# Splitting the first loads in halves and laying the two running column groups out as one piece per k-tile, in a two-layer trunk kernel

## The chip, the cores and the metric

The kernel runs on one core of a Trainium2 chip. The metric is the device time of one execution in microseconds. TensorE multiplies, VectorE and ScalarE do elementwise work and read accumulators, GpSimd is all but unused, and SyncE (SP) issues every DMA from one queue, in the order of the program.

## The reference

A decoder trunk of two layers works on 256 tokens of width 2048, in float32. The begin of the kernel, which the change touches, is the modulated input of layer 0 and its first product:

```python
def _adaln(c, w, b):
    mod = jax.nn.silu(c) @ w + b
    shift, scale, gate = jnp.split(mod, 3, axis=-1)
...
h = x * (1 + scale) + shift          # layer 0
proj = h @ in_w                      # 2048 x 10304: z 4096, x 4096, B 1024, C 1024, dt 64
z, xBC, dt = jnp.split(proj, ...)
xBC = silu(causal_depthwise_conv(xBC))
...                                  # chunked state-space scan, gated RMSNorm, y @ out_w
```

Behind it come a shared key/value product, a layer of dilated window attention, and two layer norms.

## The kernel before, in words

**Precision and pieces.** Each product of float32 matrices is done in three passes over operands split in a high and a low half. A weight piece `raw` is 128x1024 (512 KB): for the products here 2 k-tiles of 128 rows, 512 columns each. `load_piece` fetches it, `split` makes `whi` on ScalarE (L99) and `wlo` on VectorE (L101). `cm_piece` (L125 to L127) takes the weights as the stationary operand: 24 matmuls of 128x256 for a piece, 12 for each k-tile. `tm_piece` (L173 to L175) has the tokens as the stationary operand: 12 matmuls of 128x512.

**The stage at the begin (0 to about 187 us).** It makes h, k-tile by k-tile (16 of them), and at the same time starts products with the k-tiles that are there. `c` is broadcast to all partitions and goes through SiLU (`cb_`, L68). For each k-tile, two loads `araw` (128x2048, 1024 KB; scale and shift) are multiplied by `cb_` and summed along the row by one instruction of VectorE, the dot (`ada_dot`, L251); `ada_bias` adds the bias table `adab` (L256); `htmp` (L413) applies scale and shift to x on ScalarE; `actT` (L414) is h's high half and L415 its low half, on VectorE. `xt` holds x for two k-tiles. `h_step` is one dot with what follows from it; it is called a set number of times for each weight piece.

**The written order.** The pieces are worked in an order written out as rows of words:

```python
for row in ("b4:0. b6:0. h z2:0. b2:0 x1:0 h", "b2:1. x1:1. z1:0 z1:1. z4:0 h h",
```

`b4:0` is piece 0 of a product that was begun for column group b4; a dot ends what is accumulated for now, and `put_away` copies or adds the accumulators to SBUF (L486, L488). `h` stands for the two running column groups (the first bc group and the first xs group), whose accumulators `first` stay in PSUM for the whole stage: an `h` takes the next piece of one group or of the other, in turn, so that each piece covers two k-tiles of one group. `fetch_piece` issues the load of the next piece in this order, `fetch` that of the next `araw`; both go into SP's one queue. `split` is called one piece ahead. After the stage the convolutions of the two running groups are done (`conv`, L320 and L323).

Of the kernel before, what the change touches and what calls it, by code (L numbers as in the profile page):

```python
# [13 lines left out]
ALU = mybir.AluOpType  # L14
# [35 lines left out]
def trunk(ctx, tc, xT, x, c, par, cst, bias, lnrow, ada, wdt, win, wxs, wout, wk, wv, wbin, wbout, out):  # L50
# [16 lines left out]
    bcast(cb_, c)  # L67
    S.activation(cb_, cb_, AF.Silu)  # L68
# [221 lines left out]
    with ExitStack() as cA:  # L290
# [14 lines left out]
        with ExitStack() as cS:  # L305
# [4 lines left out]
            begun = {("z", 0): (win[6], 6, szt[0]), ("z", 1): (win[7], 4, szt[1]),  # L310
                     ("xs", 1): (win[5], 4, as_cm(y[0])), ("bc", 2): (win[1], 4, as_cm(y[1])),
                     ("z", 2): (win[8], 14, y[2]), ("bc", 4): (win[2], 12, as_cm(y[3])), ("z", 4): (win[10], 6, y[4]),
                     ("bc", 6): (win[3], 12, as_cm(y[5])), ("z", 6): (win[12], 10, y[6]), ("z", 5): (win[11], 8, y[7])}
# [39 lines left out]
            def product(kind, g, pre=None):  # L353

                if kind == "xs" and g > 1:
                    return xs_wide(g)

                src, k0, part = begun.get((kind, g), (None, 0, None))
                if src is None:
                    src = win[{"bc": g // 2, "xs": 4 + g, "z": 6 + g}[kind]]  # L360
                if kind == "z":
                    ps = tm_chunk(src, hh_, hl_, rate=R, k0=k0, pre=pre)
                    if g not in sz:
                        sz[g] = p0.tile([P, 2, 512], F32, name="sz")
                    for b in range(2):
                        if part is not None:
                            V.tensor_tensor(part[:, b, :], ps[b], part[:, b, :], op=ALU.add)
                        S.activation(sz[g][:, b, :], part[:, b, :] if part is not None else ps[b], AF.Silu)
                    return
                ps = cm_quad(src, hhi, hlo, rate=R, k0=k0)  # L370
                t = tiles(ps)
                if part is not None:
                    for w in range(2):
                        V.tensor_tensor(part[:, 2 * w:2 * w + 2, :], ps[w], part[:, 2 * w:2 * w + 2, :], op=ALU.add)
                    t = [part[:, n, :] for n in range(4)]
                if kind == "xs":
                    xs_conv(g, t)
                else:
                    bc_conv(g, t)

            with ExitStack() as c0:
# [6 lines left out]
                def fetch():  # L388
                    i = len(raws)
                    if i < len(cols):  # L390
                        raws.append(ada_load((wp1, pe)[i // 2 % 2], *cols[i]))

# [4 lines left out]
                def h_step():  # L397
# [6 lines left out]
                    ada_dot(0, kind, kt, raw)  # L404
                    if kt > 1:
                        pin[0] = None
                    fetch()
                    while late:
                        late.pop()()
                    if kind == "shift":  # L410
                        ada_bias(0, slice(kt, kt + 1), slice(0, 2))
                        t = pe.tile([P, L], F32, name="htmp")
                        S.activation(t, xts[kt // 2][:, kt % 2, :], AF.Identity, bias=shift(0, kt), scale=scale(0, kt))  # L413
                        S.activation(hhi[:, kt, :], t, AF.Copy)  # L414
                        late.append(lambda: V.tensor_tensor(hlo[:, kt, :], t, hhi[:, kt, :].bitcast(F32),  # L415
                                                            op=ALU.subtract))
# [7 lines left out]
                for row in ("b4:0. b6:0. h z2:0. b2:0 x1:0 h", "b2:1. x1:1. z1:0 z1:1. z4:0 h h",  # L424
# [10 lines left out]
                source = {"dt": wdt, -2: win[0], -1: win[4], **{n: p[0] for n, p in zip(names, begun.values())}}  # L435
                pss = {-2: first[0], -1: first[1]}
# [53 lines left out]
                begin, done, ended, halves = {}, set(), [], {}  # L490
                for i, (k, q, ends) in enumerate(order):
                    fetch_piece()
                    if i == 16:
# [11 lines left out]
                    z = str(k)[0] == "z"  # L505
# [4 lines left out]
                    if z:  # L510
# [527 lines left out]
def _layout(x, c, ada_w, ada_b, ln_g, ln_b, a_in_w, a_conv_w, a_conv_b, a_dt_bias,  # L1038
# [29 lines left out]
    def mask(delta, win_, dil):  # L1068
# [11 lines left out]
    win = _pieces(np.concatenate([bc, xs[:, :1024], z], 1))  # L1080
# [3 lines left out]
        "ada": ada, "wdt": _dt(dt), "win": win, "wxs": _pieces(xs[:, 1024:], 256, 4),  # L1084
# [23 lines left out]
```

## Time and profile before

| | |
|---|---|
| median of 3 runs | 1255.73 us (1254.37 to 1255.77) |
| profiled execution | 1254.31 us |
| its span, first to last instruction | 1252.5 us |
| TensorE busy | 1218.5 us (97%) |
| VectorE busy | 1032.4 us (82%) |
| ScalarE busy | 702.1 us (56%) |
| granted TensorE clock, mean | 0.998 |
| first matmul | 14.96 us after the span's start |

Times in the profile are counted from the span's first instruction. A row of a timeline has the start, the duration, the engine, the line of the source, the operation, and in brackets how long the engine was idle before it and what it waited for.

### The profile page before, as it was taken

The numbers are of one execution on the slowest core, as the hardware profiler recorded it, in microseconds if no ns is written. First come the engines' busy times: TensorE is split into PE (matmuls) and PEld (weight loads), VectorE is DVE, ScalarE is ACT, GpSimd is POOL, SyncE is SP. The second block draws the span as 40 slices with busy tenths as digits, with TensorE's granted clock in tenths as the row PEclk, the third lists the DMA queues.
The fourth block names the chain that finished last, engine by engine and source line by source line (L and its number), as shares of the span: only waits on it lengthen the run. The fifth ranks groups of instructions, "written<-read, shape, count | busy, mean of one in ns | idle before, by whom it ended". The sixth has DMA issues, their size and how long they took to land.

```text
span 1252.5 us, 18746 instructions
## 1 busy us (share of the span) xinstructions
PE 1218.5 (97%) x7086; PEld 1042.7 (83%) x7086; DVE 1032.4 (82%) x1466; ACT 702.1 (56%) x1039; POOL 0.2 (0%) x4
## 2 busy tenths in 40 slices
PE   4999999999999999999999999999999999999997
PEld 4989998898888878788888788888888888888886
DVE  6999986999987989899777778879888866758777
ACT  3655577869588789653444444434445644445631
POOL 0000000000000000000000000000000000000000
PEclk9999999999999999999999999999999999999999
DMA  9999977677556546699898569989998774464741
GB/s 381 422 421 423 420 252 261 225 274 286 201 169 225 171 159 202 223 328 358 335 323 298 174 192 383 363 315 344 364 389 309 229 248 136 132 203 120 228 177 67
DMA packets 80586, 335.88 MB, mean 268 GB/s; under 512 B 9104, under 2 KB 9328, under 8 KB 67696
## 3 DMA queue, kind: packets, MB, share of 16 engines
q1 hardware_dynamic: 80496, 334.69, 73.9%
q8 instruction: 55, 0.90, 0.3%
q14 instruction: 35, 0.29, 0.1%
HBM read 332.47 MB, written 2.18 MB: 267 GB/s over the span
## 4 chain that ended last, share of the span: by engine, by line
PE 86%; DVE 5%; DMA 5%; issue 2%; ACT 1%; SPq 0%; DVEq 0%; ACTq 0%
PE acc L149 20%; PE acc L174 13%; PE acc L175 13%; PE acc L173 13%; PE acc L152 10%; PE acc L125 3%; PE acc L127 3%; PE acc L126 3%; DMA raw<-in_wk 2%; DVE wlo L101 1%; PE py L625 1%; DMA raw<-in_win 1%; DVE araw L251 1%; DMA araw<-in_ada 1%; DMA raw<-in_wv 1%
## 5 line engine op out<-in xcount | busy, mean ns | idle before, releaser
L99 ACT ACTIVATE whi<-raw 128x1024 fp32r<-128x1024 f32 x392 | 412.1, 1058 | 386.0 <-PE acc L175 151.4
L101 DVE TENSOR_TENSOR wlo<-raw,whi 128x1024 fp32r<-128x1024 f32 x392 | 473.5, 1221 | 145.3 <-ACT whi L99 141.1
L149 PE MATMUL acc<-actT,whi 128*128 128x512 f32 x1280 | 405.2, 397 | 0.0
L152 PEld LDWEIGHTS acc<-actT,wlo 128*128 128x128 f32 x1280 | 238.9, 188 | 62.8 <-DVE wlo L101 8.2
L174 PE MATMUL acc<-wlo,actT 128*128 128x512 f32 x688 | 270.0, 392 | 0.6 <-DVE wlo L101 0.5
L173 PE MATMUL acc<-whi,actT 128*128 128x512 f32 x688 | 266.6, 394 | 1.2 <-ACT actT L681 1.2
L152 PE MATMUL acc<-actT,wlo 128*128 128x256 f32 x1280 | 253.7, 280 | 4.5 <-DVE wlo L101 3.7
L251 DVE SCALAR_TENSOR_TENSOR araw<-araw,cb__72 128x2048 f32<-128x2048 f32 x96 | 219.3, 2285 | 9.5 <-DMA araw<-in_ada 9.3
L149 PEld LDWEIGHTS acc<-actT,whi 128*128 128x128 f32 x1280 | 195.8, 189 | 0.4
L175 PE MATMUL acc<-whi,actT 128*128 128x512 f32 x432 | 168.8, 391 | 0.0
L174 PEld LDWEIGHTS acc<-wlo,actT 128*128 128x128 f32 x688 | 129.3, 188 | 28.5 <-DVE wlo L101 2.8
L173 PEld LDWEIGHTS acc<-whi,actT 128*128 128x128 f32 x688 | 128.8, 188 | 27.2 <-ACT actT L681 1.7
L125 PE MATMUL acc<-actT,whi 128*128 128x256 f32 x384 | 108.9, 288 | 17.6 <-ACT actT L414 17.5
L126 PE MATMUL acc<-actT,whi 128*128 128x256 f32 x384 | 109.5, 287 | 0.0
L127 PE MATMUL acc<-actT,wlo 128*128 128x256 f32 x384 | 107.3, 287 | 1.2 <-DVE wlo L101 1.2
L175 PE MATMUL acc<-whi,ylo 128*128 128x512 f32 x256 | 100.7, 393 | 0.0
L175 PEld LDWEIGHTS acc<-whi,actT 128*128 128x128 f32 x432 | 81.1, 188 | 16.6
L125 PEld LDWEIGHTS acc<-actT,whi 128*128 128x128 f32 x384 | 74.3, 194 | 18.6 <-ACT actT L414 17.7
L126 PEld LDWEIGHTS acc<-actT,whi 128*128 128x128 f32 x384 | 75.1, 196 | 0.3
L127 PEld LDWEIGHTS acc<-actT,wlo 128*128 128x128 f32 x384 | 73.9, 196 | 1.6 <-DVE wlo L101 1.6
L175 PEld LDWEIGHTS acc<-whi,ylo 128*128 128x128 f32 x256 | 48.1, 188 | 9.7
L583 ACT ACTIVATE seg<-cbc,cumT 128x128 f32<-128x128 f32 x128 | 41.2, 389 | 5.0 <-PE py L625 4.9
(257 smaller groups left out, 1061.7 us busy)
## 6 DMA issues: line engine op xcount, KB each, us to landing
araw<-in_ada SPq DMA_DIRECT2D x96, 1024.0 KB, 7.3
raw<-in_win SPq DMA_DIRECT2D x112, 512.0 KB, 6.1
raw<-in_wout SPq DMA_DIRECT2D x64, 512.0 KB, 5.2
raw<-in_wbin SPq DMA_DIRECT2D x64, 512.0 KB, 4.2
raw<-in_wxs SPq DMA_DIRECT2D x48, 512.0 KB, 4.5
raw<-in_wv SPq DMA_DIRECT2D x48, 512.0 KB, 5.9
raw<-in_wk SPq DMA_DIRECT2D x48, 512.0 KB, 8.0
cbc<-cumd SPq DMA_DIRECT2D x16, 512.0 KB, 5.1
```

Of the source, the lines that this page charges most:

```text
L99: copied.append(S.activation(hi, raw, AF.Copy))
L101: latest.append(V.tensor_tensor(lo, raw, hi.bitcast(F32), op=ALU.subtract))
L125: T.matmul(o, hi[:, k, c_], ahi[:, kt, :], start=first, stop=False, skip_group_check=True)
L126: T.matmul(o, hi[:, k, c_], alo[:, kt, :], start=False, stop=False, skip_group_check=True)
L127: T.matmul(o, lo[:, k, c_], ahi[:, kt, :], start=False, stop=kt == k1 - 1, skip_group_check=True)
L149: T.matmul(ps[n], hi[:, k, n * P:n * P + P], both(kt), start=kt == 0, stop=False, skip_group_check=True)
L152: T.matmul(ps[n][:, 0, :], lo[:, k, n * P:n * P + P], high(kt), start=False, stop=kt == KT - 1, skip_group_check=True)
L173: T.matmul(o, h_, hi[:, k, :], start=kt == k0, stop=False, skip_group_check=part)
L174: T.matmul(o, h_, lo[:, k, :], start=False, stop=False, skip_group_check=part)
L175: end = T.matmul(o, l_, hi[:, k, :], start=False, stop=kt == k1 - 1, skip_group_check=part)
L251: V.scalar_tensor_tensor(raw, raw, 1.0, cb_, op0=ALU.mult, op1=ALU.mult, accum_out=mod[layer][:, ct, j:j + 1])
L583: S.activation(seg[:, hh, b, :], cbc[:, hh, b, :], AF.Relu, bias=cumT[:, b, h0 + hh:h0 + hh + 1], scale=-1.0)
```

## The change

1. `c` is fetched and put through SiLU in two halves of 1024 columns.
2. The two `araw` loads of k-tile 0 are fetched in halves, and their dots are done in halves (`first_dot`). The first halves go to a small tile `ahead`, and one more add puts them together.
3. The pieces of the two running groups come from a new array `whead`: a piece is one k-tile of both groups (1024 columns) instead of two k-tiles of one. `head_piece` does its 24 matmuls. The first row of the order begins with an `h`, and its last `h` goes.
4. The first weight piece, now of `whead`, is fetched ahead of `xt` and `adab`; its two halves (`top`) are made outside the loop, the high one ahead of `htmp` of k-tile 0 on ScalarE, the low one by VectorE after the first two steps.
5. In the first four `h_step`s the next `araw` is fetched after the step instead of inside it, and the order of weight and `araw` loads is another: behind the first 20 loads each `araw` has one weight piece more ahead of it.

```diff
-    bcast(cb_, c)
-    S.activation(cb_, cb_, AF.Silu)
+    HALF = [slice(0, D // 2), slice(D // 2, D)]
+    for h in HALF:
+        bcast(cb_[:, h], c, h.start)
+    for h in HALF:
+        S.activation(cb_[:, h], cb_[:, h], AF.Silu)
...
+                def first_dot(kind, raw):
+                    j = KIND.index(kind)
+                    for h, to in zip(HALF, (ahead[:, j:j + 1], mod[0][:, 0, j:j + 1])):
+                        V.scalar_tensor_tensor(raw[:, h], raw[:, h], 1.0, cb_[:, h], op0=ALU.mult, op1=ALU.mult,
+                                               accum_out=to)
...
                     if kind == "shift":
                         ada_bias(0, slice(kt, kt + 1), slice(0, 2))
+                        if kt == 0:
+                            V.tensor_tensor(mod[0][:, 0, 0:2], mod[0][:, 0, 0:2], ahead, op=ALU.add)
                         t = pe.tile([P, L], F32, name="htmp")
-                        S.activation(t, xts[kt // 2][:, kt % 2, :], AF.Identity, bias=shift(0, kt), scale=scale(0, kt))
+                        with tc.issue_after(copied[0].ins) if kt == 0 else ExitStack():
+                            S.activation(t, xts[kt // 2][:, kt % 2, :], AF.Identity, bias=shift(0, kt),
+                                         scale=scale(0, kt))
...
-                for row in ("b4:0. b6:0. h z2:0. b2:0 x1:0 h", "b2:1. x1:1. z1:0 z1:1. z4:0 h h",
+                for row in ("h b4:0. b6:0. h z2:0. b2:0 x1:0", "b2:1. x1:1. z1:0 z1:1. z4:0 h h",
...
-                            n = -2 if sum(o[0] == -2 for o in order) == sum(o[0] == -1 for o in order) else -1
-                            order.append((n, sum(o[0] == n for o in order), False))
+                            order.append((two, sum(o[0] == two for o in order), False))
...
                 fetch()
                 fetch()
+                fetch_piece()
                 fetch_x(0)
                 nc.sync.dma_start(adab_, par[:, :NB])
                 V.tensor_scalar(adab[:, :, :, 1:3], adab[:, :, :, 1:3], 1.0, None, op0=ALU.add)
-                fetch_piece()
+                fetch()
                 fetch_piece()
                 fetch()
                 fetch_piece()
-                for _ in range(2):
+                fetch_piece()
+                top = [wp.tile([P, 1024], F32R, name=n, bufs=4) for n in ("whi", "wlo")]
+                copied.append(S.activation(top[0], pieces[0], AF.Copy))
+                for i in range(2):
                     for _ in range(2):
-                        h_step()
+                        h_step(False)
                     while late:
                         pin[0] = late.pop()().ins
+                    if i == 0:
+                        latest.append(V.tensor_tensor(top[1], pieces[0], top[0].bitcast(F32), op=ALU.subtract))
+                    fetch()
                     fetch_piece()
+
+                def head_piece(kt, w):
+                    hi, lo = w
+                    for a in range(2):
+                        for n in range(4):
+                            o, c_ = first[a][n // 2][:, n % 2, :], slice(512 * a + n * P, 512 * a + n * P + P)
+                            T.matmul(o, hi[:, c_], hhi[:, kt, :], start=kt == 0 and n % 2 == 0, stop=False,
+                                     skip_group_check=True)
+                            T.matmul(o, hi[:, c_], hlo[:, kt, :], start=False, stop=False, skip_group_check=True)
+                            T.matmul(o, lo[:, c_], hhi[:, kt, :], start=False, stop=kt == KT - 1, skip_group_check=True)
...
                 for i, (k, q, ends) in enumerate(order):
                     fetch_piece()
+                    if i == 2:
+                        fetch()
...
-    win = _pieces(np.concatenate([bc, xs[:, :1024], z], 1))
+    win = _pieces(np.concatenate([bc[:, 512:], xs[:, 512:1024], z], 1))
+    whead = _pieces(np.concatenate([bc[:, :512], xs[:, :512]], 1), 1024, 1)[0]
```

A scheduler decides the final order on each engine, and numbers behind a name are those of its buffers. Line numbers move by 3 and more in the changed kernel: L101 becomes L104, L251 becomes L254, L256 becomes L259, L415 becomes L440, L323 becomes L326, L486 becomes L528; L407 is `first_dot`, L434 the added add, L473 the 1 added to the scale's bias, L487 the first low half.

SP's queue from the first load on, before: `cb__72` is c, `in_ada` the dots' data, `in_win` weight pieces.

```order
L63 DMA cb__72<-in_c 128x2048
L244 DMA araw_126<-in_ada 128x2048
L244 DMA araw_128<-in_ada 128x2048
L395 DMA xt_130<-in_xT 128x512
L447 DMA adab_75<-in_par 128x96
L93 DMA raw_134<-in_win 128x1024
L93 DMA raw_136<-in_win 128x1024
L244 DMA araw_138<-in_ada 128x2048
L93 DMA raw_140<-in_win 128x1024
L244 DMA araw_143<-in_ada 128x2048
L244 DMA araw_146<-in_ada 128x2048
L93 DMA raw_153<-in_win 128x1024
```

The same place now:

```order
L63 DMA cb__72<-in_c 128x1024 x2
L396 DMA araw_129<-in_ada 128x1024 x2
L396 DMA araw_132<-in_ada 128x1024 x2
L96 DMA raw_135<-in_whead 128x1024
L412 DMA xt_137<-in_xT 128x512
L472 DMA adab_77<-in_par 128x96
L247 DMA araw_141<-in_ada 128x2048
L96 DMA raw_143<-in_win 128x1024
L247 DMA araw_145<-in_ada 128x2048
L96 DMA raw_147<-in_win 128x1024
L96 DMA raw_149<-in_whead 128x1024
L247 DMA araw_165<-in_ada 128x2048
```

One weight piece moved ahead of `xt` and `adab`, the data of dots 2 and 3 (the second k-tile) stand ahead of the second and third piece, and a third piece stands ahead of dot 4's data.

VectorE from its first dot to the low half of the second k-tile of h, before: `mod0_84` takes the dots, L415 is h's low half.

```order
L251 SCALAR_TENSOR_TENSOR araw_126,mod0_84<-araw_126,cb__72 128x2048
L251 SCALAR_TENSOR_TENSOR araw_128,mod0_84<-araw_128,cb__72 128x2048
L448 TENSOR_SCALAR adab_75<-adab_75 128x32x2
L256 TENSOR_TENSOR mod0_84<-mod0_84,adab_75 128x2
L101 TENSOR_TENSOR wlo_171<-raw_134,whi_170 128x1024
L415 TENSOR_TENSOR actT_88<-htmp_149,actT_88 128x256
L101 TENSOR_TENSOR wlo_175<-raw_136,whi_174 128x1024
L251 SCALAR_TENSOR_TENSOR araw_138,mod0_84<-araw_138,cb__72 128x2048
L101 TENSOR_TENSOR wlo_207<-raw_140,whi_206 128x1024
L251 SCALAR_TENSOR_TENSOR araw_143,mod0_84<-araw_143,cb__72 128x2048
L256 TENSOR_TENSOR mod0_84<-mod0_84,adab_75 128x2
L415 TENSOR_TENSOR actT_88<-htmp_162,actT_88 128x256
```

VectorE's first rows now, as far as the first dot of the second k-tile:

```order
L407 SCALAR_TENSOR_TENSOR araw_129,ahead_128<-araw_129,cb__72 128x1024
L407 SCALAR_TENSOR_TENSOR araw_129,mod0_86<-araw_129,cb__72 128x1024
L407 SCALAR_TENSOR_TENSOR araw_132,ahead_128<-araw_132,cb__72 128x1024
L407 SCALAR_TENSOR_TENSOR araw_132,mod0_86<-araw_132,cb__72 128x1024
L487 TENSOR_TENSOR wlo_152<-raw_135,whi_151 128x1024
L473 TENSOR_SCALAR adab_77<-adab_77 128x32x2
L259 TENSOR_TENSOR mod0_86<-mod0_86,adab_77 128x2
L434 TENSOR_TENSOR mod0_86<-mod0_86,ahead_128 128x2
L440 TENSOR_TENSOR actT_90<-htmp_160,actT_90 128x256
L254 SCALAR_TENSOR_TENSOR araw_141,mod0_86<-araw_141,cb__72 128x2048
```

The first low half of weights moved ahead of everything that needs `adab`, and the one or two splits that stood ahead of dot 2 are gone from there.

VectorE at the end of the stage, before, around the low half of the weight piece next to be used (`wlo_1950`); `s2_97` are accumulators put away, `cacc` is the convolution.

```order
L323 SCALAR_TENSOR_TENSOR cacc_1872<-acc_125,prm_76,cacc_1872 128x253
L486 TENSOR_TENSOR s2_97<-acc_1546,s2_97 128x512
L486 TENSOR_TENSOR s2_97<-acc_1547,s2_97 128x512
L323 SCALAR_TENSOR_TENSOR cacc_1878<-acc_125,prm_76,cacc_1878 128x255
L543 TENSOR_SCALAR araw_1895<-araw_1895 128x128
L323 SCALAR_TENSOR_TENSOR cacc_1878<-acc_125,prm_76,cacc_1878 128x254
L545 SCALAR_TENSOR_TENSOR araw_1895<-araw_1895 128x128
L323 SCALAR_TENSOR_TENSOR cacc_1878<-acc_125,prm_76,cacc_1878 128x253
L545 SCALAR_TENSOR_TENSOR araw_1895<-araw_1895 128x128
L101 TENSOR_TENSOR wlo_1950<-raw_1947,whi_1949 128x1024
```

The same place now, where that piece's low half is `wlo_1958`:

```order
L326 SCALAR_TENSOR_TENSOR cacc_1868<-acc_126,prm_78,cacc_1868 128x254
L591 SCALAR_TENSOR_TENSOR araw_1903<-araw_1903 128x128
L326 SCALAR_TENSOR_TENSOR cacc_1868<-acc_126,prm_78,cacc_1868 128x253
L591 SCALAR_TENSOR_TENSOR araw_1903<-araw_1903 128x128
L104 TENSOR_TENSOR wlo_1958<-raw_1955,whi_1957 128x1024
L528 TENSOR_TENSOR s2_99<-acc_1556,s2_99 128x512
L528 TENSOR_TENSOR s2_99<-acc_1557,s2_99 128x512
L326 SCALAR_TENSOR_TENSOR cacc_1874<-acc_126,prm_78,cacc_1874 128x255
L326 SCALAR_TENSOR_TENSOR cacc_1880<-acc_127,prm_78,cacc_1880 128x255
```

The two adds and part of the convolution moved behind the low half.

More of the change, by code (lines that the diff above doesn't have):

```diff
@@ L434, in trunk @@
                 order[-5:-5] = [("dt", 0, False), ("dt", 1, False)]
-                source = {"dt": wdt, -2: win[0], -1: win[4], **{n: p[0] for n, p in zip(names, begun.values())}}
-                pss = {-2: first[0], -1: first[1]}
+                source = {"dt": wdt, two: whead, **{n: p[0] for n, p in zip(names, begun.values())}}
+                pss = {}
                 pieces = []
@@ L488, in put_away @@
                                 S.activation(place, ps[w], AF.Copy)
-                begin, done, ended, halves = {}, set(), [], {}
+                begin, done, ended, halves = {}, set(), [], {0: top}
                 for i, (k, q, ends) in enumerate(order):
                     fetch_piece()
+                    if i == 2:
+                        fetch()
                     if i == 16:
@@ L509, in trunk @@
                     k0, k1 = (begin[k], 2 * q + 2 if ends else KT) if k in part else (0, KT)
-                    if z:
+                    if k == two:
+                        head_piece(q, [t if i == 0 else t.rearrange("p k n -> p (k n)") for t in halves[i]])
+                    elif z:
                         tm_piece(source[k], q, pss[k], hh_, hl_, k0=k0, k1=k1, w=halves[i])
```

33 lines of the change are left out of this document (21 added, 12 removed).

## The prediction

> **What bounds the kernel now.** I read the page first: busy times (its part 1) and the chain that ended last (its part 4).
>
> ```profile
> PE 1218.5 (97%) x7086; PEld 1042.7 (83%) x7086; DVE 1032.4 (82%) x1466; ACT 702.1 (56%) x1039; POOL 0.2 (0%) x4
> PE 86%; DVE 5%; DMA 5%; issue 2%; ACT 1%; SPq 0%; DVEq 0%; ACTq 0%
> ```
>
> TensorE is busy for 1218.5 of 1252.5 us, so only some 34 us of idle time are to be had in the whole kernel. The change removes no matmul; it can gain only where TensorE waits. The waits of TensorE in the first 36 us, and the table by stage (length; busy time and instructions of PE, PEld, DVE, ACT, POOL; granted clock; DMA share; GB/s), say how much of it lies at the begin:
>
> ```profile
> PE acc L125 <- ACT actT L414: 17.5, 2, 15.0
> 0.00:15.00 15.00, 0.04 (x1) 0.04 (x1) 5.41 (x9) 5.25 (x6) 0.20 (x4) 1.00 0.87 335
> 15.00:22.00 7.00, 6.58 (x36) 5.91 (x36) 6.83 (x7) 1.91 (x2) 0.00 (x0) 1.00 1.01 425
> 22.00:25.40 3.40, 0.89 (x7) 0.81 (x7) 2.25 (x5) 1.02 (x2) 0.00 (x0) 1.00 1.02 425
> 25.40:28.90 3.50, 3.50 (x19) 3.50 (x18) 2.98 (x4) 2.63 (x4) 0.00 (x0) 0.53 1.00 423
> 40.00:60.00 20.00, 20.00 (x137) 18.57 (x136) 18.24 (x21) 12.49 (x17) 0.00 (x0) 1.00 1.02 420
> ```
>
> Half of the idle time is 17.5 us of waiting for the first two tiles of h (L414 writes their high half). DMA runs at 425 GB/s throughout, VectorE is nearly full, and from 40 us on TensorE is too. So the begin is bound by the order in which transfers arrive, and behind them by VectorE. TensorE's own timeline shows the places (start, duration, the idle time before):
>
> ```profile
> 14.96 0.80 PE L125 MATMUL acc<-actT,whi 128*128 128x256 f32 x2 [14.96 <-ACT actT L414]
> 17.05 0.41 PE L126 MATMUL acc<-actT,whi 128*128 128x256 f32 x1
> 17.27 0.41 PE L127 MATMUL acc<-actT,wlo 128*128 128x256 f32 x1
> 21.68 0.28 PE L126 MATMUL acc<-actT,whi 128*128 128x256 f32 x1
> 21.80 0.28 PE L127 MATMUL acc<-actT,wlo 128*128 128x256 f32 x1
> 24.59 0.39 PE L125 MATMUL acc<-actT,whi 128*128 128x256 f32 x1 [2.51 <-ACT actT L414]
> 30.49 0.40 PE L173 MATMUL acc<-whi,actT 128*128 128x512 f32 x1
> 33.24 0.28 PE L125 MATMUL acc<-actT,whi 128*128 128x256 f32 x1
> 34.76 0.39 PE L127 MATMUL acc<-actT,wlo 128*128 128x256 f32 x1 [0.89 <-DVE wlo L101]
> 48.77 0.63 PE L173 MATMUL acc<-whi,actT 128*128 128x512 f32 x2
> ```
>
> At full clock a 128x256 matmul starts every 0.12 us (21.68, 21.80), so a piece of 24 costs 2.88; a token-major piece costs 2.75 (30.49 to 33.24). Early matmuls start 0.21 apart (17.05, 17.27), and the clock falls to 0.53 in 25.4–28.9, after a stretch in which TensorE was busy for 0.89 of 3.40 us. The row at 48.77 begins the tenth piece, z1:0. The nine before it, eight of 2.88 and one of 2.75, cost 25.8 without loss; they took 48.77 − 14.96 = 33.8. So 8.0 us are lost after the first matmul, beside 14.96 ahead of it. How much earlier z1:0 starts is my measure of the change.
>
> **What stands ahead of the first matmul.** Rows of the chain, of VectorE's and ScalarE's timelines, and of the DMA issues (KB each):
>
> ```profile
> 1.63 8.63 DMA araw<-in_ada
> 12.73 0.16 DVE L256 TENSOR_TENSOR mod<-mod,adab 128x2 f32<-128x2 f32 x1
> 12.93 0.60 ACT L413 ACTIVATE htmp<-xt,mod 128x256 f32<-128x256 f32 x1 [5.62 <-DVE mod L256]
> 13.54 1.06 ACT L99 ACTIVATE whi<-raw 128x1024 fp32r<-128x1024 f32 x1
> 18.49 1.06 ACT L99 ACTIVATE whi<-raw 128x1024 fp32r<-128x1024 f32 x1 [2.64 <-DMA raw<-in_win]
> 30.80 1.06 ACT L99 ACTIVATE whi<-raw 128x1024 fp32r<-128x1024 f32 x1 [0.93 <-DMA raw<-in_win]
> 32.06 1.06 ACT L99 ACTIVATE whi<-raw 128x1024 fp32r<-128x1024 f32 x1 [0.20 <-DMA raw<-in_win]
> 20.95 2.29 DVE L251 SCALAR_TENSOR_TENSOR araw<-araw,cb__72 128x2048 f32<-128x2048 f32 x1
> 37.56 2.29 DVE L251 SCALAR_TENSOR_TENSOR araw<-araw,cb__72 128x2048 f32<-128x2048 f32 x1 [0.26 <-DMA araw<-in_ada]
> 40.73 0.42 ACT L414 ACTIVATE actT<-htmp 128x256 fp32r<-128x256 f32 x1
> araw<-in_ada SPq DMA_DIRECT2D x11, 1024.0 KB, 13.0
> raw<-in_win SPq DMA_DIRECT2D x13, 512.0 KB, 12.7
> xt<-in_xT SPq DMA_DIRECT2D x2, 256.0 KB, 11.1
> adab<-in_par SPq DMA_DIRECT2D x1, 48.0 KB, 9.5
> ```
>
> Everything goes through SP's one queue, and arrivals follow its order. At 425 GB/s 1024 KB take 2.47 us and 512 KB 1.23; the splits at 30.80 and 32.06, both released by a transfer, are 1.26 apart. So I get each arrival of the changed kernel by adding sizes to an arrival of before.
>
> **First h: nothing gained.** *Halving.* Now the second dot starts when araw 1 is there (1.63 + 8.63 = 10.26) and ends 2.29 later, at 12.6. In halves, three of the four are done before the last half lands at 10.26, and the last takes about 2.29/2 + 0.1: ends 11.5. That is worth 1.1 us if nothing else stood there. *Added adds and split.* adab now comes behind the first weight piece (512 KB) as well. Its arrival is not shown: xt and adab are 304 KB, 0.7 us by size, but the split at 18.49 came 8.2 us after araw 1 with 2864 KB between, which is 6.9 by size, so small rows cost up to 1.3 us more. araw 1 at 10.26 + 1.23 + 0.7 to 2.0 = 12.2 to 13.5; I take the late end, as the only row that measures this stretch includes that loss. VectorE's first wlo fits before it (raw at 11.5, whi 1.06, wlo 1.22: ends 13.8). Then three small operations on the dots (one more than now; about 0.16 each by the row at 12.73, 0.5 in all), htmp 0.60, actT 0.42, and a hand-over between engines: first matmul at 15.4, 0.4 to 0.5 later than 14.96. The early adab gives the same, since wlo holds VectorE until 13.8 anyway; without that split ahead it would be 1 us earlier, so the split eats what the halves bring. The low half of h is ready directly behind, and the first piece is already split, so nothing waits for wlo.
>
> **Second h: 1.2 us earlier, and more work ahead of it.** araw 3 is dot 3's data. Before it now stand c, three araw, three raw, xt and adab; dot 3 starts at 20.95. In the changed order 3888 KB lie between araw 1 and the third raw, 1024 KB more than in the 2864 that ended at 18.49: that raw lands at 20.96, and araw 3, just ahead of it, at 19.7. Dot 3 to first matmul took 24.59 − 20.95 = 3.64, so second-h matmuls start at 23.35. Until then TensorE has 24 + 12 matmuls of kt 0 and 4 of the next piece, 40 instead of 36, since whead has all its 24 for kt 0. Starting at 15.4 with the same 0.21 pitch until about 19.2, they end near 22.0. Gap: 1.3 instead of 2.51. In such a gap TensorE is busy for over 2 of 3.4 us, not 0.89, so I take the 25.4–28.9 throttle (3.5 us at 0.53, a loss of 1.7) to be gone.
>
> **To z1:0.** From 23.35: 32 left-over matmuls of b4 and b6 (3.8), whead 1 (2.88), z2:0 (2.75), b2:0 and x1:0 (5.76), and the kt 2 halves of b2:1 and x1:1 (2.88): 41.4. Then comes what is late next: **the fourth h.** Before its araw 7 the queue now holds one raw more. The bytes that ended at 30.80 (fifth raw) end with the seventh in the new order, then 512 + 256 + 1024 + 512 KB: at the same byte, 13360 KB, the old row has dot 7 released at 37.56, the new one its ninth raw. 1024 KB later araw 7 is there: 40.0. By size alone from 32.06 it would be 38.8 (the old stretch to 37.56 took 1.1 us longer than its bytes); I take 40.0 as the stretch is the same. Dot to actT's end was 40.73 + 0.42 − 37.56 = 3.6: h at 43.6. TensorE waits 2.2 us, does the two kt 3 halves (2.88), and starts z1:0 at 46.5 instead of 48.77. **Lead: 2.3 us**; with araw 7 at 38.8 it is 3.5, with the pessimistic sums above 1.9.
>
> **Does the lead hold?** From 40 us TensorE has no gap, and the lead needs every later piece 2.3 us earlier. Behind the begin each raw stands one place further ahead of the araws, and VectorE splits one piece more per dot count: the split of a piece takes the place of the one before it. A tight pair:
>
> ```profile
> 99.33 1.23 DVE L101 TENSOR_TENSOR wlo<-raw,whi 128x1024 fp32r<-128x1024 f32 x1
> 101.46 1.23 DVE L101 TENSOR_TENSOR wlo<-raw,whi 128x1024 fp32r<-128x1024 f32 x1 [0.52 <-ACT whi L99]
> 104.45 0.39 PE L174 MATMUL acc<-wlo,actT 128*128 128x512 f32 x1
> ```
>
> The split at 101.46 ends 1.76 ahead of its use; in the earlier place it would end 2.1 sooner, and use is 2.3 sooner: 1.6 left. So a lead of 2.3 holds, one of 3.5 not everywhere. The last dots (h, dt) are far ahead of their pieces.
>
> **End of the begin.** One stall of TensorE stands there:
>
> ```profile
> 186.35 1.37 DVE L486 TENSOR_TENSOR s<-acc,s 128x512 f32<-128x512 f32 x2
> 189.34 1.22 DVE L101 TENSOR_TENSOR wlo<-raw,whi 128x1024 fp32r<-128x1024 f32 x1
> 189.55 0.61 PE L173 MATMUL acc<-whi,actT 128*128 128x512 f32 x2
> 190.62 0.50 PE L174 MATMUL acc<-wlo,actT 128*128 128x512 f32 x1 [0.45 <-DVE wlo L101]
> ```
>
> At 0.23 a matmul (2.75 for 12) the third was due at 190.0 and came at 190.62: 0.6 us lost. The two adds of 1.37 are now behind that wlo, and so are several convolution steps; but both first groups now end with the very last h piece, where the bc group ended one piece (2.88) sooner, so convolutions start later. I take 0.5 of the 0.6; bounds 0 and 0.6. Until 460 us the order differs only in details under full TensorE: 0, bounds ±1.
>
> **Sum.** On the profiled execution, 1254.31 (span 1252.5 and 1.8 around it): 1254.31 − 2.3 − 0.5 = 1251.5. The three runs have 1254.37 to 1255.77 with a median of 1255.73, 1.4 above the profiled one; measured from there 2.8 less is **1252.9**.
>
> **The rivals.** *A throttle after the new gap.* The wait at 41.4–43.6 is 2.2 us; the old one of 2.51 was followed by 3.5 us at 0.53. Against it:
>
> ```profile
> 464.00:470.00 6.00, 3.92 (x24) 3.20 (x23) 6.00 (x9) 5.97 (x10) 0.00 (x0) 1.00 0.58 207
> ```
>
> Here some 2 us are idle and the clock stays 1.00. If it falls, 1.7 us go: gain 1.1, 1254.6. The Trainium skill ("TensorE: Matmul & The Clock Gate", HAM oscillation) warns only of idle gaps over about 3.4 us; by that this gap costs nothing, but the old throttle after 2.51 us shows that shorter ones can cost. Chance 0.18.
>
> *The lead is eaten by feeding.* In 40–60 us DMA runs at 420 GB/s and VectorE has under 2 us of 20 free; if a split comes 1.5 to 2.3 late once, TensorE falls back to the old pace: gain 0 to 0.8, 1255.3. Chance 0.11.
>
> *Slower: the convolutions crowd the end.* Around 172–190 us VectorE and ScalarE do the first groups' convolutions between splits. If the late bc group pushes the wlo of 189.34 back by its full piece, the stall is 0.6 + 2.88 = 3.5, longer than the gap of 2.51 that brought the throttle: 1.7 more. With the low lead of 1.9: 1255.7 − 1.9 + 2.9 + 1.7 = 1258.4. It decides once that wlo comes 1.9 us later against TensorE than now. For it: the rows at 186.35 and 189.34 show VectorE at other work between splits; against it: the wlo now stands ahead of the adds. Chance 0.14.
>
> *The halves cost a transfer each.* Three DMAs more, and the first matmul hangs on them. By the rows at 30.80 and 32.06 another one costs 0.03 us beyond its bytes. At the dearest, each costs what the small rows cost, 1.3: the first matmul is 3.9 later and the gain gone, 1256.8. The Trainium skill ("DMA: Bandwidth & Descriptors", Anatomy of one DMA) gives about 2 us fixed for a transfer on GpSimd's path, which would be 6 us; queued as here, the rows show none of it. Chance 0.02.
>
> **How the numbers follow.** My forecast has 0.53, and 0.02 goes to a new wait after 190 us that no row shows. About 0.2% (2.5 us) is what a measurement of this kernel can tell from no change: below 1253.2 is faster, above 1258.2 slower. The forecast lies close to that line: 0.45 of its 0.53 is faster, 0.08 same. The throttle gives 0.01 faster and 0.17 same, feeding 0.11 same, the crowded end 0.02 same and 0.12 slower, the halves 0.02 same, the unseen wait 0.02 slower: faster 0.46, same 0.40, slower 0.14. The range goes from a lead of 3.1 with the whole stall of 0.6, on a run 1.1 below the median, 1250.9, to 1257.4, which leaves out only the worst of the crowded end.
>
> **What would show it.** Right: first matmul (L497) at 15.0–15.5; the next gap 1.0–1.6 us and no half clock behind it; dot 7 released at about 40; a gap of about 2 us before the kt 3 halves; z1:0 at 46–47; no stall until 185; the begin's last piece 2 to 2.8 us earlier than 189.55. Wrong: a granted clock near 0.5 between 42 and 48; waits for wlo or actT between 50 and 180; or a stall over 2 us near 187.

## The result, and the profile after

| kernel | median, us | lowest to highest | ratio to before, 95% interval |
|---|---|---|---|
| before | 1255.64 (6 runs) | 1254.37 to 1255.77 | |
| changed | 1260.42 (6 runs) | 1257.59 to 1262.09 | 1.0041 [1.0031, 1.0052] |

The changed kernel is 4.8 us slower; the forecast was 2.8 faster. The profiled execution of the changed kernel took 1260.64, its span is 1258.9, 6.4 more than before. TensorE's busy time (page, part 1) and chain (part 4) hardly show it:

```profile
PE 1220.5 (97%) x7086; PEld 1044.7 (83%) x7086; DVE 1032.5 (82%) x1471; ACT 701.3 (56%) x1038; POOL 0.2 (0%) x4
PE 84%; DMA 7%; DVE 6%; issue 1%; ACT 1%; SPq 0%; DVEq 0%; ACTq 0%
```

The place shows once the same matmul is looked up in both timelines of TensorE. In the changed kernel the first matmul, the second h, the fourth h, z1:0, the scan matmuls of group 0, and two later waits read:

```profile
16.62 0.79 PE L497 MATMUL acc<-actT,whi 128*128 128x256 f32 x2 [16.62 <-ACT actT L439]
24.09 0.50 PE L128 MATMUL acc<-actT,whi 128*128 128x256 f32 x2 [0.35 <-ACT actT L439]
43.88 0.74 PE L128 MATMUL acc<-actT,whi 128*128 128x256 f32 x4 [1.44 <-ACT actT L439]
46.85 0.40 PE L176 MATMUL acc<-whi,actT 128*128 128x512 f32 x1
216.47 0.60 PE L616 MATMUL aux<-bcm 128*128 128x256 f32 x2
222.87 0.69 PE L671 MATMUL py<-xd,seg 128*64 128x64 f32 x16 [1.12 <-DVE seg L632]
224.40 0.69 PE L671 MATMUL py<-xd,seg 128*64 128x64 f32 x16 [0.84 <-DVE seg L632]
226.87 2.05 PE L662 MATMUL aux<-xo,cb 128*128 128x512 f32 x2 [1.79 <-DVE xo L650]
471.21 0.50 PE L155 MATMUL acc<-actT,wlo 128*128 128x256 f32 x2 [2.08 <-DVE wlo L104]
547.35 0.44 PE L723 MATMUL aux<-cc,s 128*128 128x128 f32 x2 [2.07 <-DVE ylo L728]
```

and of before, at the last places that answer to these:

```profile
219.22 0.60 PE L570 MATMUL aux<-bcm 128*128 128x256 f32 x2
229.53 1.15 PE L625 MATMUL py<-xd,seg 128*64 128x64 f32 x30
467.08 0.50 PE L152 MATMUL acc<-actT,wlo 128*128 128x256 f32 x2 [2.08 <-DVE wlo L101]
```

z1:0 starts 1.9 us earlier than before (46.85 against 48.77), and the first matmul of the scan (`aux<-bcm`, 219.22 before) 2.7 earlier, at 216.47. The same wait ends at 467.08 before and at 471.21 now: 4.1 later. So the begin gained what was hoped for and 6.9 us went between 216 and 471. The table of this stage shows all of it inside 20 us (the changed kernel first, with two more stretches that are used below; then before):

```profile
215.00:235.00 20.00, 16.11 (x121) 12.24 (x120) 19.26 (x30) 14.87 (x26) 0.00 (x0) 0.83 0.38 120
226.00:227.00 1.00, 0.13 (x1) 0.16 (x1) 1.00 (x3) 0.00 (x0) 0.00 (x0) 0.54 0.00 0
464.00:480.00 16.00, 13.92 (x94) 11.55 (x93) 15.19 (x23) 13.95 (x29) 0.00 (x0) 0.89 0.69 206
```

```profile
215.00:235.00 20.00, 20.00 (x164) 16.88 (x163) 18.69 (x29) 14.67 (x26) 0.00 (x0) 1.00 0.49 170
```

TensorE is idle for 3.9 us. A mean clock of 0.83 over 20 us is a half clock (0.50) for 6.8 us; it begins at about 226.1, inside the last of the waits, so 6.0 us of it fall on work and cost 3.0 more: 6.9 in all. In the profiled execution the half clock behind the old gap at 469 costs another 1.8 (0.89 of 16), and at 547 a wait that goes back to one late `araw` 2.1; waits of 0.3 to 0.4 us at 1008, 1017 and 1165 are gone.

Why TensorE runs dry there is in VectorE's timeline. Before:

```profile
215.64 1.23 DVE L101 TENSOR_TENSOR wlo<-raw,whi 128x1024 fp32r<-128x1024 f32 x1 [5.31 <-ACT whi L99]
217.53 2.36 DVE L101 TENSOR_TENSOR wlo<-raw,whi 128x1024 fp32r<-128x1024 f32 x2 [0.67 <-ACT whi L99]
219.81 1.28 DVE L374 TENSOR_TENSOR s<-acc,s 128x512 f32<-128x512 f32 x2
```

Now:

```profile
215.39 1.23 DVE L104 TENSOR_TENSOR wlo<-raw,whi 128x1024 fp32r<-128x1024 f32 x1 [8.00 <-ACT whi L102]
216.53 1.28 DVE L377 TENSOR_TENSOR s<-acc,s 128x512 f32<-128x512 f32 x2
218.80 2.88 DVE L326 SCALAR_TENSOR_TENSOR cacc<-s,prm,cacc 128x255 f32<-128x255 f32 x7
226.04 0.68 DVE L650 TENSOR_TENSOR xo<-aux,dec 128x512 f32<-128x512 f32 x1
228.23 2.35 DVE L104 TENSOR_TENSOR wlo<-raw,whi 128x1024 fp32r<-128x1024 f32 x2
```

From the row of `s<-acc,s` on, VectorE works for 12 us at the convolution of the next x group and at the operands of the first scan, without a split between. Before the change three splits stood ahead of this block, and TensorE had 38 matmuls of weight pieces (0.23 us each) to do behind the scan's transposes until its operands came. In the changed kernel one split stands ahead; the scheduler put the scan's own matmuls (`py`, L671) behind 14 matmuls, and the other splits at 228.23, behind the block. TensorE, 2.7 us early, comes to `py` at about 221.7 and waits for `seg`, then for `xo`.

### The profile page after: what moved, and what is told of

The parts are those of the page before. It is cut to its first block, busy times and chain, and to the rows that moved or that the text cites. A ratio compares the mean times of both kernels' runs of the same rounds, so it can differ in the third digit from the quotient of the medians.

```text
span 1258.9 us, 18753 instructions
## 1 busy us (share of the span) xinstructions
PE 1220.5 (97%) x7086; PEld 1044.7 (83%) x7086; DVE 1032.5 (82%) x1471; ACT 701.3 (56%) x1038; POOL 0.2 (0%) x4
## 4 chain that ended last, share of the span: by engine, by line
PE 84%; DMA 7%; DVE 6%; issue 1%; ACT 1%; SPq 0%; DVEq 0%; ACTq 0%
PE acc L152 20%; PE acc L178 13%; PE acc L177 13%; PE acc L176 13%; PE acc L155 10%; DMA araw<-in_ada 3%; DMA raw<-in_wk 2%; DVE araw L254 2%; PE acc L128 2%; PE acc L129 2%; PE acc L130 2%; DVE wlo L104 1%; DMA raw<-in_win 1%; PE py L671 1%; PE acc L500 1%
## 5 line engine op out<-in xcount | busy, mean ns | idle before, releaser
L104 DVE TENSOR_TENSOR wlo<-raw,whi 128x1024 fp32r<-128x1024 f32 x391 | 472.6, 1221 | 141.6 <-ACT whi L102 137.5
L155 PEld LDWEIGHTS acc<-actT,wlo 128*128 128x128 f32 x1280 | 239.6, 189 | 61.5 <-DVE wlo L104 6.6
L155 PE MATMUL acc<-actT,wlo 128*128 128x256 f32 x1280 | 254.4, 280 | 3.8 <-DVE wlo L104 3.6
L254 DVE SCALAR_TENSOR_TENSOR araw<-araw,cb__72 128x2048 f32<-128x2048 f32 x94 | 214.8, 2285 | 7.0 <-DMA araw<-in_ada 6.9
L152 PEld LDWEIGHTS acc<-actT,whi 128*128 128x128 f32 x1280 | 196.6, 189 | 0.5
L128 PE MATMUL acc<-actT,whi 128*128 128x256 f32 x256 | 71.9, 285 | 1.8 <-ACT actT L439 1.8
L129 PE MATMUL acc<-actT,whi 128*128 128x256 f32 x256 | 71.8, 283 | 0.0
L130 PE MATMUL acc<-actT,wlo 128*128 128x256 f32 x256 | 71.0, 283 | 0.0
L497 PE MATMUL acc<-actT,whi 128*128 128x256 f32 x128 | 35.1, 291 | 16.6 <-ACT actT L439 16.6
L128 PEld LDWEIGHTS acc<-actT,whi 128*128 128x128 f32 x256 | 48.8, 192 | 2.5 <-ACT actT L439 2.2
L129 PEld LDWEIGHTS acc<-actT,whi 128*128 128x128 f32 x256 | 49.0, 192 | 0.1
L130 PEld LDWEIGHTS acc<-actT,wlo 128*128 128x128 f32 x256 | 48.5, 192 | 0.0
```

What stands on the lines that cost most here:

```text
L104: latest.append(V.tensor_tensor(lo, raw, hi.bitcast(F32), op=ALU.subtract))
L128: T.matmul(o, hi[:, k, c_], ahi[:, kt, :], start=first, stop=False, skip_group_check=True)
L129: T.matmul(o, hi[:, k, c_], alo[:, kt, :], start=False, stop=False, skip_group_check=True)
L130: T.matmul(o, lo[:, k, c_], ahi[:, kt, :], start=False, stop=kt == k1 - 1, skip_group_check=True)
L152: T.matmul(ps[n], hi[:, k, n * P:n * P + P], both(kt), start=kt == 0, stop=False, skip_group_check=True)
L155: T.matmul(ps[n][:, 0, :], lo[:, k, n * P:n * P + P], high(kt), start=False, stop=kt == KT - 1, skip_group_check=True)
```

## The experiments

The theory S was that this later order, not the begin, costs the time; the rival B, that it is the begin's new phase, by chance waits further on. I first moved only TensorE's side. The ratio of each experiment is to runs of the kernel before taken together with it; the median of before lay between 1254.85 and 1255.77 in them, so medians of different experiments are compared with that in mind. The diffs show the main lines of each edit, with comments that explain; `tc.issue_after(x)` orders an instruction behind `x`.

**scan_later.** The changed kernel, with TensorE's scan matmuls held behind the third piece of z1:

```diff
+                with tc.issue_after(held[g].ins) if g in held else ExitStack():
-                T.matmul(po, cb[:, 2, :], xo, start=True, stop=True)
+                    T.matmul(po, cb[:, 2, :], xo, start=True, stop=True)
...
+                    if g == 0:
+                        held[0] = zend[2]          # last matmul of z1's third piece
```

> The changed kernel with one addition: the first scan group's own matmuls (po and py of group 0) may not be issued on TensorE before the third weight piece of z1. Theory S (the later order): the begin keeps its lead of 1.9 us at z1:0, and the changed kernel loses it again at 221 to 229 us, because those matmuls now stand behind only 14 matmuls of weight pieces where before 38 filled the time until VectorE had their operands. Then the stall of some 5.5 us and the half clock behind it vanish: 1252.5 to 1255. Theory B (the loss comes from the begin's new phase, by chance waits and throttles later): no change, 1258 to 1261.

Measured: 1264.43 us, ratio 1.0071 [1.0056, 1.0086]; slower still. The wait only changed its name (TensorE's timeline):

```profile
230.09 0.80 PE L177 MATMUL acc<-wlo,actT 128*128 128x512 f32 x1 [7.76 <-DVE wlo L104]
```

With the scan out of the way TensorE asks for the second piece of z1, whose low half stands behind VectorE's block: 7.8 us. Neither S as I had put it nor B foresaw this. It says where to look: while VectorE's order stays, another order on TensorE only changes what TensorE waits for.

**before_scan_early.** The kernel before, with the scan's matmuls behind 12 matmuls of pieces, and the further pieces of z1 behind them:

```diff
+                if g == 0:
+                    rs = stage2(g, *st1)
                 if g < G - 2:
                     product("z", g + 1)           # from its second piece on: issue_after(last py matmul)
```

> The kernel before, with the order of the first scan group as in the changed one: its matmuls stand behind 12 matmuls of weight pieces instead of 38, and the later pieces of z1 wait for them. Nothing else is altered. Theory S: TensorE runs dry at about 223 us and waits for VectorE until 230, with a half clock behind it: 6 to 9 us slower than before, 1261 to 1265. Theory B: within 1.5 us of before.

Measured: 1264.37, 1.0068 [1.0051, 1.0085]: 9.5 us slower, with the begin of before untouched. The wait is the foreseen one:

```profile
229.56 1.98 PE L627 MATMUL py<-xd,seg 128*64 128x64 f32 x32 [4.77 <-DVE xd L598]
```

Here VectorE kept the order of before, with three low halves ahead of its block:

```profile
216.78 1.23 DVE L101 TENSOR_TENSOR wlo<-raw,whi 128x1024 fp32r<-128x1024 f32 x1 [5.30 <-ACT whi L99]
218.67 2.36 DVE L101 TENSOR_TENSOR wlo<-raw,whi 128x1024 fp32r<-128x1024 f32 x2 [0.67 <-ACT whi L99]
```

So the later order on TensorE alone makes a kernel slow; the begin is not needed for it. With scan_later it says that both engines must be right: the low halves made ahead of VectorE's block, and their matmuls placed ahead of the scan's own. In the profile the stage accounts for 6.7 of the loss (5.0 idle, a mean clock of 0.91 over 20 us); the rest was not traced.

**halves_alone.** The kernel before with c, SiLU and the first dots in halves:

> The kernel before with c, its SiLU and the first dots in halves, and nothing else; the order at the first scan stays as before (38 matmuls ahead). Theory H (more transfers cost time): the second araw lands some 1.1 us later than the 10.26 of before, as in the changed kernel, the first matmul comes 0 to 1 us later, time +0 to +1.5: 1255.5 to 1257. Theory G (the halves let the dots start early for nothing): first matmul about 1 us earlier, 14.0, time 1254 to 1255.

Measured: 1256.09, 1.0012 [1.0001, 1.0022], hardly clear of the noise. The first matmul is at 15.66 instead of 14.96, but here it waits for the high half of the weights, which ScalarE now makes behind h. What the halves do to arrivals is seen where nothing else at the begin differs: ScalarE's first split of a weight piece, which starts when the piece has landed, in the changed kernel and in splits_ahead_no_halves (below).

```profile
12.68 1.06 ACT L480 ACTIVATE whi<-raw 128x1024 fp32r<-128x1024 f32 x1 [5.50 <-DMA raw<-in_whead]
```

```profile
11.77 1.06 ACT L463 ACTIVATE whi<-raw 128x1024 fp32r<-128x1024 f32 x1 [4.25 <-DMA raw<-in_whead]
```

In the profiles with this order of loads, that split starts at 12.5 to 13.3 with halves (four kernels) and at 11.7 to 11.8 without (four). The third piece of halves_alone lands at 19.25, against 18.49 before. The dots gain nothing either. VectorE's dots of the first k-tile, here (the first and the last half) and before (the second whole one):

```profile
8.05 1.23 DVE L407 SCALAR_TENSOR_TENSOR araw<-araw,cb__72 128x1024 f32<-128x1024 f32 x1 [7.05 <-DMA araw<-in_ada]
11.76 1.23 DVE L407 SCALAR_TENSOR_TENSOR araw<-araw,cb__72 128x1024 f32<-128x1024 f32 x1
```

```profile
10.29 2.29 DVE L251 SCALAR_TENSOR_TENSOR araw<-araw,cb__72 128x2048 f32<-128x2048 f32 x1
```

The first half dot starts at 8.05, no earlier than the whole one did (7.92), and the last ends at 13.0 against 12.6. Theory H holds in its sign: the halves cost a little and bring nothing.

**scan_later_no_halves.** scan_later with c, SiLU and the first dots whole. Expected by Theory H: first matmul at 15.4 to 15.6, and 0.5 to 1.2 us below scan_later, which was then put at 1252.5 to 1255; by Theory G: first matmul at 16.6 or later, and no gain. Measured: 1262.10, 1.0061 [1.0041, 1.0080], with the first matmul at 15.44 instead of 17.27 and z1:0 at 46.46 instead of 47.33. The begin went by H; the median is 2.3 below scan_later's, but its six runs spread from 1260.43 to 1266.50, and the wait for a low half (7.75 at 229.47) is still there.

**splits_ahead.** The changed kernel, with two pieces of z1 fetched and split before the scan block is written:

```diff
                 ps = cm_quad(src, hhi, hlo, rate=R, k0=k0)
+                if (kind, g) == ("xs", 1):
+                    z1, k1, _ = begun["z", 1]
+                    for q in range(k1 // 2, k1 // 2 + 2):
+                        early[q] = split(load_piece(z1[q]))
```

> The changed kernel with one addition at the later place: the first two weight pieces of z1 are fetched and split before the scan work of group 0 is written, so that VectorE makes their low halves ahead of the block of convolution and scan work at 216 to 228 us; on TensorE 38 matmuls of pieces then stand ahead of the scan's own, as before the change. Holding TensorE's side alone only turned the wait for the scan's operands into one of 8.1 us for a low half. Theory S2 (the loss is VectorE's order at this place): no gap of more than 1.5 us between 215 and 235, no half clock there, the lead of the begin survives: 1252 to 1254.5. Theory B (the loss comes from elsewhere): 1258 to 1262.

Measured: 1253.62, 0.9990 [0.9977, 1.0003]; 6.8 us below the changed kernel's median, 6.4 by the ratios. The table of the stage:

```profile
215.00:235.00 20.00, 20.00 (x154) 16.35 (x154) 19.60 (x32) 16.97 (x33) 0.00 (x0) 1.00 0.56 192
```

No idle time, full clock. That is S2, and B has fallen. (The wait that the expectation calls 8.1 us is the 7.76 of scan_later's row.)

**one_split_ahead.** The same with one piece instead of two (`k1 // 2 + 1`), which leaves 26 matmuls ahead of the scan:

> The changed kernel with only the first piece of z1 split ahead instead of two; 26 matmuls of pieces then stand ahead of the scan's own on TensorE (14 in the changed kernel, 38 with two splits ahead). Theory S2 (how many pieces are split ahead of VectorE's scan block sets the stall): the stall is 12 matmuls or 2.7 us shorter than the 5.5 of the changed kernel, some 2.5 to 3.5 us at 220 to 230, with a half clock in some runs: 1255 to 1258.5, between splits_ahead and the changed kernel. Rival (only the scan's place relative to some fixed event matters): equal to one of the two.

Measured: 1257.96, 1.0018 [1.0008, 1.0028]. The stage is half mended:

```profile
215.00:235.00 20.00, 18.00 (x138) 13.97 (x137) 18.41 (x29) 15.42 (x30) 0.00 (x0) 0.91 0.49 175
```

With 14, 26 and 38 matmuls ahead TensorE is idle for 3.9, 2.0 and 0 us of these 20, at a mean clock of 0.83, 0.91 and 1.00, and the medians are 1260.42, 1257.96 and 1253.62 (ratios 1.0041, 1.0018, 0.9990). The loss goes by the number of pieces that are split ahead of VectorE's block and placed ahead of the scan.

**before_splits_ahead.** The control: the kernel before with the same addition.

> The kernel before with the same addition as in splits_ahead and nothing of the change: the control. With S2 the later order is now much the same in both, so the difference to splits_ahead is what the begin is worth, 1.9 to 2.8 us: 1254 to 1256.5 here. If this kernel is as fast as splits_ahead, the begin's lead is worth nothing in the end.

Measured: 1256.73, 1.0014 [1.0002, 1.0026]. Against 1253.62 the changed begin is worth 3.1 us when the later order is nearly alike: 38 matmuls ahead of the scan in both, though details behind it differ (this kernel waits for 1.1 us between 222 and 320, splits_ahead not at all). In the two profiles z1:0 is 2.9 apart (49.94 and 47.01), more than the 1.9 against the kernel before: here a half clock follows the wait that ends at 34.42 (a mean of 0.74 in 36–40). Against the kernel before itself, splits_ahead gains only 1.7.

**splits_ahead_no_halves.** splits_ahead with c, SiLU and first dots whole:

> As splits_ahead, with c, its SiLU and the first two dots whole. Theory H (a halved transfer costs time): first matmul near 15.5 instead of 16.6, lead at z1:0 larger by 0.3 to 1.0, time 0.3 to 1.0 below splits_ahead: 1251.5 to 1253.5. Theory G (the halves bring an earlier start): first matmul at 16.6 or later, time equal or above.

Measured: 1252.17, 0.9979 [0.9967, 0.9990], 1.45 us below splits_ahead; first matmul and z1:0 at 15.52 and 46.35 instead of 16.46 and 47.01. Theory H again, somewhat more than expected; the intervals of the two kernels overlap.

**splits_ahead_layout_and_fetch_order.** Of the begin only the layout, the row and the order of the loads are left; the first split goes back into the loop.

> As splits_ahead_no_halves, and the first weight split goes back into the loop, behind the first h on ScalarE and VectorE; what is left of the change is the layout with one piece per k-tile, its place first in the row, and the order of the loads. Theory T (the split ahead of h costs 1 us at the first matmul): first matmul at 14.3 to 14.8, but z1:0 moves by less than 0.5, since the fourth h sets it: time within 0.7 of splits_ahead_no_halves. Rival: the first matmul counts in full, 1 us faster than splits_ahead_no_halves.

Measured: 1251.52, 0.9976 [0.9966, 0.9987]: the fastest kernel of the study, 3.8 us below the 1255.28 of before beside it, though within 0.65 us of the one above. On T it says little, since the scheduler left the split where it was (VectorE's timeline):

```profile
12.78 1.23 DVE L101 TENSOR_TENSOR wlo<-raw,whi 128x1024 fp32r<-128x1024 f32 x1 [0.16 <-ACT whi L99]
13.92 0.19 DVE L455 TENSOR_SCALAR adab<-adab 128x64 f32<-128x64 f32 x1
```

The first matmul stays at 15.44. What the split ahead of h costs was not measured.

**layout_alone.** The kernel before with one piece per k-tile of both groups and nothing else:

> The kernel before with the layout alone: one piece per k-tile of both running groups, the row of pieces, the loads' order, the transfers and the first split as before. The order at the first scan flips here already: 26 matmuls ahead of it instead of 38. Theory S2: the begin gains 1 to 1.5 us (48 instead of 36 matmuls of the first k-tile ahead of the second h) and a stall of some 2.5 to 3.5 us comes at 220 to 230: 1255 to 1258. Rival (the flip needs the moved loads): no stall there, 1253.5 to 1255.

Measured: 1260.14, 1.0033 [1.0019, 1.0046]. The order at the scan has flipped here (26 ahead), as S2 says and its rival denies, and there are waits of 1.9 and 0.5 us. But the begin gained nothing, z1:0 being at 50.14 in this profile, so the time missed the range on the slow side.

**splits_ahead_layout.** The same with the two splits ahead:

> layout_alone with two pieces of z1 split ahead, 38 matmuls ahead of the scan again. Theory S2: no stall at 215 to 235, the layout's gain of 1 to 1.5 us is kept: 1253 to 1255; splits_ahead_layout_and_fetch_order, which has the loads moved as well (the second h 1.2 us earlier), is 0.5 to 1.5 us faster than this. Rival: the order of the loads is worth nothing, both the same within 0.5.

Measured: 1255.87, 0.9999 [0.9989, 1.0009], above the range. TensorE's wait and z1:0:

```profile
34.52 0.39 PE L127 MATMUL acc<-actT,wlo 128*128 128x256 f32 x1 [1.92 <-DVE wlo L101]
48.54 0.63 PE L173 MATMUL acc<-whi,actT 128*128 128x512 f32 x2
```

The layout's 12 more matmuls for the first k-tile are there (48 ahead of the second h), but TensorE only comes earlier to a low half that is ready no sooner: the wait for it ends at 34.52 here and at 34.69 in layout_alone, and with the old layout at 34.76 in the kernel before, 34.42 in before_splits_ahead and 35.53 in before_scan_early. That z1:0 is at 50.14 in layout_alone and at 48.54 here, with one and the same begin, is the clock behind this wait (layout_alone first):

```profile
36.00:40.00 4.00, 4.00 (x28) 4.00 (x28) 3.50 (x4) 1.14 (x2) 0.00 (x0) 0.75 1.02 422
```

```profile
36.00:40.00 4.00, 4.00 (x35) 4.00 (x35) 3.32 (x4) 1.02 (x1) 0.00 (x0) 1.00 1.03 427
```

The moved loads are worth 2.3 us at z1:0 (46.24 in splits_ahead_layout_and_fetch_order) and 4.3 in the medians, 2.9 by the ratios, where 0.5 to 1.5 had been expected.

**splits_ahead_fetch_order.** before_splits_ahead with the order of the loads alone:

> before_splits_ahead with the order of the loads alone taken from the change: the first weight piece ahead of xt and adab, one weight piece more ahead of each araw, no new layout, no halves, no split ahead of h. 36 matmuls of the first k-tile stand ahead of the second h where the layout has 48, worth 1.4 us at the second h. Theory F (the begin's gain is the order of the loads, since the fourth h sets z1:0): second h at about 23.4, wait at the fourth h about 0.5 us instead of 1.7 to 1.9, z1:0 at 46.3 to 47.3, time within 1 us of splits_ahead_layout_and_fetch_order: 1251.5 to 1253. Rival L (the layout's 12 matmuls count in full): z1:0 at 47.7 or later, 1253 to 1254.5.

```profile
43.40 0.74 PE L125 MATMUL acc<-actT,whi 128*128 128x256 f32 x4 [0.33 <-ACT actT L419]
46.38 0.40 PE L173 MATMUL acc<-whi,actT 128*128 128x512 f32 x1
```

At the begin Theory F is right: the second h at 23.28, a wait of 0.33 us at the fourth h, z1:0 at 46.38 (with 28 matmuls ahead of the second h, not 36). Up to z1:0 the gain of the begin is the order of the loads. The time does not show it: it is 1257.27, 1.0021 [1.0008, 1.0033], and missed both ranges. The later order came out another way once more, with 38 matmuls ahead of the scan but other waits (180 to 320 us):

```profile
PE aux L604 <- DVE cb L583: 2.0, 1, 2.0
PE acc L152 <- DVE wlo L101: 1.2, 1, 1.2
PE acc L174 <- DVE wlo L101: 0.5, 2, 0.3
```

## Why the prediction was wrong

**The step that failed** is one sentence: "Until 460 us the order differs only in details under full TensorE: 0, bounds ±1." It was drawn from the absence of waits before, not from the places where operands are made. The order of instructions showed 14 matmuls ahead of the scan's own instead of 38, and one low half ahead of VectorE's block instead of three; with the trace of before (`py` at 229.53, the block's length) that would have been priced at 24 matmuls of 0.23, 5.5 us, and a half clock behind it. It measured 3.9 idle and 3.0 of half clock on work, 6.9 where the sum had 0 ±1. What came is the "new wait after 190 us that no row shows", which had been given a chance of 0.02.

**The slow rival** had the right kind of mechanism (convolution and other VectorE work crowding out a split, then a half clock), but it was put at 172–190 us, where the order had improved. No wait is left there: the stall of 190.62 is gone, for which I had counted 0.5.

**The begin** went nearly by the sum, with one term off. The first matmul came at 16.62, not 15.4: I gave the halves no price. The first weight piece landed at 12.68 instead of 11.5, so its low half, which stands ahead of all that needs `adab`, ended at 15.0 instead of 13.8; that is the whole 1.2. Nor were three of the four half dots done by 10.26: the first started at 7.45, the last at 11.37, and it ended at 12.6, as before the change. The second h was at 24.09 (23.35 forecast); since TensorE started later with the same 40 matmuls, it had less of a gap, 0.35 instead of 1.3. No half clock followed, as said. The fourth h came at 43.88 (43.6), z1:0 at 46.85 (46.5); the lead of 1.9 against 2.3 lies at the low bound given. It held to the stage's end and grew to 2.7 by 216, where 2.8 had been summed up. The control puts the begin at 3.1. That "the split eats what the halves bring" stays open; that the halves bring nothing was shown. "VectorE is nearly full" was read too freely (5.41 us of the first 15, 2.25 of 3.40 at 22–25.4), but no term of the sum hangs on it.

**The rivals of the begin.** No throttle followed the wait at the fourth h, which was 1.44 and not 2.2. The feeding kept up: between z1:0 and 200 us TensorE is never idle. The halves cost a transfer each, in small: three more transfers, about 1 us, some 0.3 each, where I had read 0.03 from the rows at 30.80 and 32.06 and put the dearest at 1.3. The Trainium skill ("DMA: Bandwidth & Descriptors", Anatomy of one DMA) gives about 2 us fixed for a transfer on GpSimd's path; three would make 6, an estimate from that figure, and the trace agrees with the sign alone.

**What is not settled** is why the scheduler chooses the other order: layout_alone shows that the layout is enough to turn it, and splits_ahead_fetch_order that the loads' order turns it in another way. Nor is it shown how much of the begin's lead of 1.9 to 2.9 us is the chance of a half clock in the old begin: each of the profiles with the old order of loads has one between 24 and 40 us except splits_ahead_layout's, none with the new order has.

## What to carry to other kernels

When a change reorders a begin, the order of every later place where one engine does a long block of work for another has to be counted again: how much work does TensorE have in hand until the block is done? A stretch without waits is no proof of slack, since a few splits on the right side of a block can be what keeps it full. To judge a begin by itself, pin the later place, and run the old kernel with the same pin as a control.

## What the hardware showed that I had not expected

Several short gaps did what I ascribed to one long one: with waits of 1.1, 0.8 and 1.8 us within 222–227 the clock was at half for 6.8 us, from inside the last of them (a mean of 0.66 in 225–235):

```profile
225.00:235.00 10.00, 8.21 (x53) 5.88 (x50) 9.65 (x14) 5.56 (x13) 0.00 (x0) 0.66 0.41 123
```

The Trainium skill ("TensorE: Matmul & The Clock Gate", HAM oscillation) states as the rule that no idle gap of TensorE should be over about 3.4 us; here no single one is over 2, and the clock fell all the same. And one and the same gap of 2.1 us, which ends between 463.9 and 476.2 in all fourteen kernels, is followed by a half clock in eight of the profiles (0.89 of 464–480 in the changed kernel and in splits_ahead) and not in the other six (1.00 before; of splits_ahead_no_halves, where the gap ends at 463.91, below):

```profile
464.00:480.00 16.00, 16.00 (x92) 14.01 (x93) 15.68 (x32) 15.49 (x28) 0.00 (x0) 1.00 0.80 269
```

Each such event is worth some 1.7 us of a time; it may be part of the spread of some 5 us that kernels such as splits_ahead have from run to run (1250.78 to 1256.24), which was not tested.
